# Scale, norm weights, division, epsilon and cosine product in the attention chains of a two-layer mixer kernel

## The chip, the cores and the metric

The kernel runs on one core of a Trainium2 chip. TensorE (PE) multiplies matrices, VectorE (DVE), ScalarE (ACT) and GpSimd (POOL) do the elementwise work, SyncE (SP) issues the loads. The metric is the device time of one execution in microseconds; the median of the runs counts.

## The reference, cut to what matters

Two layers, 256 latent tokens and 256 context tokens of 1024 features. A projection of the normed tokens feeds four branches: a differential attention (a), a pooling (b), a neighbourhood attention (c) and a spatial gating (d). Their outputs are projected, gated, summed and added to the tokens; a SwiGLU follows. The last layer needs only the latents' output. What the change touches is the two attentions:

```
def _rmsnorm(t, g):
    n = t * lax.rsqrt(jnp.mean(t * t, axis=-1, keepdims=True) + EPS)
    return n * g
# a: queries and keys per half head of 64, normed with their weights; latents rotated
aq = _rope(_diff_heads(xcol(OFF_AQ, A_W), ga_q), cos_a, sin_a)
s  = jnp.einsum('bhcqd,bhckd->bhcqk', q, k) * (A_DH ** -0.5)      # 1/8
p  = jax.nn.softmax(s, axis=-1)
a  = p[:, :, 0] - lam * p[:, :, 1]
# c: queries and keys normed, not rotated; bias and mask on the local scores
cq = _rmsnorm(split_c(xcol(OFF_CQ, C_W)), gc_q)
s_loc = jnp.einsum(...) * scale + bias                            # scale = 1/8
p = jax.nn.softmax(jnp.concatenate([s_loc, s_ctx], axis=-1), axis=-1)
out = p_loc @ v_loc + p_ctx @ v_ctx
```

## The kernel before

**Products.** Every large product takes both factors in two parts, hi and lo, and adds hi·hi, lo·hi and hi·lo. `split_weights` (L217 to L232) loads 512 KB of weights on SyncE's queue (`w_raw`), ScalarE rounds them to `w_hi` (L230), VectorE subtracts to get `w_lo` (L127); three buffers of each rotate. `by_token` (L234) keeps activations stationary and streams 512 columns of weights for each of two to four tiles of 128 tokens (products `pt`); `by_feature` (L275) makes the transposed kind (`pf`). All their matmuls have line L124.

**Queries and keys.** `qk_consumer` (L379) takes a finished tile `pt`, 128 tokens by 8 heads of 64. ScalarE copies it to `qn` and squares it, VectorE reduces the squares to `hms` (L386), and `rsqrt_eps` (L147) lets GpSimd add epsilon (L149) and take the power −1/2 (L150), giving `hrs`. Some steps later `scale` multiplies by `hrs` on VectorE (L392). Latents' tiles of branch a are rotated: two products with the sines on VectorE (`qw`, L400), one with the cosines on GpSimd (L401), an addition on VectorE (L402); the norm weights are in these tables (`turn`). All other tiles, 20 of 28, are multiplied by the norm weights `gq` on VectorE (L404). Then `flip` transposes on TensorE (`ps_qT`, L412) and ScalarE copies to `aq`, `ak`, `cq` or `ck` (L413). `stacked` makes from these the parts for the scores (`k_stack`, `q_stack`, `q_low`).

**Attention.** `diff_attention` (L448) takes a head and 128 queries in a step: two score tiles `ps_s`, for each the negated row maximum `mx` on VectorE, its scaling by 1/8 (L470) and the exponential `e` with row sum on ScalarE (L472); VectorE combines the halves (L477), TensorE transposes (`ps_aT`, L485), and later `u` is normed (L511) and transposed (`ps_yT`, L518). `head_attention` (L544) does the same for one score tile `ps_cs` with a bias (L560), maximum `cmx` (L562), scaling (L563), exponential `ce` (L566), reciprocal of the sum `csum` (L567) and the division (L568) on VectorE, then transposes (`ps_pT`, L578), ScalarE's copy `pT` (L579) and the values (`ps_co`).

**Order.** The program is written as steps: `weave` emits a branch's steps with steps of a filler in between (products of another branch, or conditioning: `w_mod_c` on VectorE, L169), and `defer` puts off pieces of a chain by a number of steps. Under the second half of the first layer's neighbourhood attention the filler is the pooling branch, with sums over windows on GpSimd (L855 to L869). The scheduler of the framework then sets the order on each engine; an engine takes its instructions in that order and waits at each for what it needs.

Of the kernel before, what the change touches and what calls it, by code (L numbers as in the profile page):

```python
# [11 lines left out]
F32 = mybir.dt.float32  # L12
F32R = mybir.dt.float32r
AF = mybir.ActivationFunctionType
ALU = mybir.AluOpType
# [4 lines left out]
P = 128  # L20
# [10 lines left out]
# columns of w_in: those of by_token, then those of by_feature  # L31
# [8 lines left out]
def hybrid_block(ctx: ExitStack, tc: tile.TileContext, t: dict, out: bass.AP):  # L40
# [39 lines left out]
    def new_pair(name, n_tok):  # L80
        """hi and lo of [512, n_tok], in two slots or (256 tokens) in one."""
        if n_tok > SEQ:
            return new_slot(name + "_hi", F32R), new_slot(name + "_lo", F32R)
        both = slot.tile([P, 2, 4, SEQ], F32R, tag="S", name=name)
        return both[:, 0], both[:, 1]
# [4 lines left out]
    def weave(main, *fillers):  # L90
        """Emit main, with steps of the fillers ([steps, how many per step of main]) in between."""
# [19 lines left out]
    def flush(most):  # L111
        """Per step of the products: pieces that were put off long enough ago."""
# [34 lines left out]
    def rsqrt_eps(o, ms):  # L147
        n = ms.shape[-1]
        nc.gpsimd.tensor_scalar(o, ms, 1.0, EPS, op0=ALU.mult, op1=ALU.add)  # L149
        nc.gpsimd.tensor_tensor(o, o, half[:, :n], op=ALU.pow)  # L150

# [6 lines left out]
    def conditioning(l, gi):  # L158
        """Two vectors' columns: rows of the transposed w_mod times silu(c), summed in two halves."""
# [23 lines left out]
    def first_load(part):  # L183
        """The columns of w_mod for a quarter of the features of the first shift and scale, in whole slots."""
# [8 lines left out]
    def first_conditioning(part, ws):  # L193
        """A quarter of the features of the first shift and scale; even and odd rows of w_mod side by side."""
# [22 lines left out]
    def split_weights(src, into=None):  # L217
        """A piece [P, nk, nc_] of w in two parts."""
# [15 lines left out]
    def by_token(w, col, act, n_k, tiles, consume, first=None, ahead=False, pairs=False):  # L234
        """[token, column] products: activations stationary, 512 columns of w moving.
        first: tiles to finish before the others, with the parts of w kept on chip."""
# [38 lines left out]
    def by_feature(w, col, act, n_k, n_tok, consume):  # L275
        """[column, token] products: 256 columns of w stationary, activations moving."""
# [20 lines left out]
    def by_feature_pair(cols, act, n_tok):  # L297
        """Two by_feature of 1024 features, the second stream's tokens before the first's,
        with the parts of w kept on chip."""
# [25 lines left out]
    def modulated(l, g_name, v_shift, v_scale, res):  # L325
        """hs, ls and the steps: the squares of both halves and norm of a tile, then put(s, ks) for its stream's features of ks."""
# [5 lines left out]
        def squares(s, i, hf):  # L332
            """Half of a token's mean square, the second half added to the first."""
# [45 lines left out]
    def qk_consumer(name, qk, op, row, which=None, wait=2):  # L379
        def consume(i, ps):  # L380
# [9 lines left out]
            def scale():  # L390
                n3 = n.rearrange("p (g d) -> p g d", g=8)
                nc.vector.tensor_tensor(n3, n3, rs.unsqueeze(2).to_broadcast([P, 8, 64]), op=ALU.mult)  # L392
                if which is not None and i < 2:
# [7 lines left out]
                    nc.gpsimd.tensor_tensor(n3, n3, cg[:, i:i + 1, :].to_broadcast([P, 8, 64]), op=ALU.mult)  # L401
                    nc.vector.tensor_tensor(n, n, w, op=ALU.add)  # L402
                else:
                    nc.vector.tensor_tensor(n3, n3, op["gq"][:, row:row + 1, :].to_broadcast([P, 8, 64]), op=ALU.mult)  # L404
                defer(flip, wait)

            def flip():
# [5 lines left out]
                nc.scalar.copy(qk[name][:, :, i * P:(i + 1) * P], pt.rearrange("p (f n) -> p f n", f=4))  # L413
# [12 lines left out]
    def stacked(qT, kT, hp, n_q):  # L426
        """For heads 2 hp + c, from partitions 64 c on: k_hi and, on the other half, k_lo; q_hi and q_lo on both halves."""
# [675 lines left out]
```

## Time and profile before

| | us |
|---|---|
| median of three runs | 1589.87 (1589.41 to 1590.72) |
| span of the profiled execution | 1588.6 |
| TensorE busy, its matmuls | 1532.6 (96%) |
| VectorE busy | 1024.4 (64%) |
| ScalarE busy | 711.8 (45%) |
| GpSimd busy | 140.3 (9%) |

The span runs from the first to the last instruction of one profiled execution; the rest of the device time lies around it. Busy shares are means over stages of different kinds. The waits of an engine are its idle stretches, put down to the instruction that ended them. A granted clock of 1.00 is TensorE at 2.4 GHz, 0.50 at 1.2 GHz. Matmuls are pipelined, so one that is shown as 0.39 us long is followed by the next after 0.23 us.

### The profile page before, as it was taken

Reading aid. Unit: us, or ns where it says so; the run is one execution under the profiler, and the core shown is the slowest. Engines: PE = TensorE matmul, PEld = TensorE weight load, DVE = VectorE, ACT = ScalarE, POOL = GpSimd, SP = SyncE. Lnnn points to the kernel's source line nnn. Section 1 sums busy time; section 2 is a strip of 40 time slices with the busy share of each in tenths; the row PEclk is TensorE's granted clock in tenths of the full one; section 3 lists DMA queues with packets and bytes.
Section 4 is the critical chain, followed back from the end, with each engine's and each line's share of the span. In section 5 each row is a group of like instructions: output and inputs, shape, how many; then the busy total and the mean of one; then the engine's idle time right before and its main releaser. Section 6 shows DMA issues by size and latency. Waiting matters only on the chain.

```text
span 1588.6 us, 22209 instructions
## 1 busy us (share of the span) xinstructions
PE 1532.6 (96%) x8388; PEld 1300.1 (82%) x8388; DVE 1024.4 (64%) x1957; ACT 711.8 (45%) x1213; POOL 140.3 (9%) x162
## 2 busy tenths in 40 slices
PE   6989999999989999999999999999999999999998
PEld 4778887887767888888888888778978989899897
DVE  2656886556876786577555556567855896655555
ACT  4544463455643233533221233546645675454443
POOL 0220000400050000000000000130012040000000
PEclk9999999999999999999999999999999999999999
DMA  9423333232325565355555554324424535645554
GB/s 343 146 84 128 107 94 106 67 121 77 116 75 184 159 206 179 107 159 176 174 194 171 174 178 167 107 83 143 134 92 133 190 128 183 203 146 184 188 187 144
DMA packets 80988, 235.76 MB, mean 148 GB/s; under 512 B 10560, under 2 KB 13424, under 8 KB 80752
## 3 DMA queue, kind: packets, MB, share of 16 engines
q1 hardware_dynamic: 80880, 234.34, 45.3%
q8 instruction: 66, 1.08, 0.3%
q14 instruction: 42, 0.34, 0.1%
HBM read 232.18 MB, written 2.12 MB: 147 GB/s over the span
## 4 chain that ended last, share of the span: by engine, by line
PE 80%; DVE 10%; POOL 3%; ACT 3%; DMA 2%; issue 2%; SPq 0%; POOLq 0%; ACTq 0%; DVEq 0%
PE pf L124 47%; PE pt L124 26%; POOL hrs L150 2%; DVE w_lo L127 2%; PE ps_u L124 1%; PE ps_co L124 1%; PE ps_pT L578 1%; DVE w_mod_c L169 1%; PE ps_cs L124 1%; PE ps_s L124 1%; ACT w_hi L230 1%; DMA w_mod<-in_w_mod_t 1%; PE ps_nT L359 1%; DVE qn L392 1%; DVE hms L386 1%
## 5 line engine op out<-in xcount | busy, mean ns | idle before, releaser
L230 ACT CAST w_hi<-w_raw 128x1024 fp32r<-128x1024 f32 x308 | 323.5, 1051 | 546.2 <-PE pf L124 212.8
L127 DVE TENSOR_TENSOR w_lo<-w_raw,w_hi 128x1024 fp32r<-128x1024 f32 x308 | 377.6, 1230 | 276.3 <-ACT w_hi L230 272.1
L124 PE MATMUL pf<-h_hi,w_hi 128*128 128x256 f32 (+1 forms) x1344 | 450.2, 336 | 0.2 <-ACT h_hi L367 0.2
L124 PE MATMUL pf<-h_lo,w_hi 128*128 128x256 f32 (+1 forms) x1344 | 449.2, 335 | 0.0
L124 PE MATMUL pf<-h_hi,w_lo 128*128 128x256 f32 (+1 forms) x1344 | 448.7, 334 | 0.2 <-DVE w_lo L127 0.2
L124 PEld LDWEIGHTS pf<-h_lo,w_hi 128*128 128x128 f32 x1344 | 255.5, 190 | 26.3 <-issue 1.2
L124 PEld LDWEIGHTS pf<-h_hi,w_hi 128*128 128x128 f32 x1344 | 255.1, 190 | 26.6 <-ACT h_hi L367 0.7
L124 PEld LDWEIGHTS pf<-h_hi,w_lo 128*128 128x128 f32 x1344 | 255.4, 190 | 25.3 <-DVE w_lo L127 0.4
L169 DVE SCALAR_TENSOR_TENSOR w_mod_c<-w_mod,crow 128x512 f32<-128x512 f32 x256 | 169.3, 694 | 32.5 <-DMA w_mod<-in_w_mod_t 31.3
L124 PE MATMUL pt<-w_lo,h_hi 128*128 128x512 f32 x384 | 152.4, 397 | 6.9 <-DVE w_lo L127 6.9
L124 PE MATMUL pt<-w_hi,hid 128*128 128x512 f32 x496 | 154.3, 390 | 0.0
L124 PE MATMUL pt<-w_hi,h_lo 128*128 128x512 f32 x384 | 151.4, 395 | 1.0 <-DVE h_lo L127 1.0
L124 PE MATMUL pt<-w_hi,h_hi 128*128 128x512 f32 x384 | 152.0, 400 | 0.1
L124 PEld LDWEIGHTS pt<-w_hi,hid 128*128 128x128 f32 x496 | 93.2, 188 | 19.4
L124 PE MATMUL pt<-w_lo,hid 128*128 128x512 f32 x248 | 96.5, 389 | 0.0
L124 PEld LDWEIGHTS pt<-w_lo,h_hi 128*128 128x128 f32 x384 | 72.9, 190 | 23.8 <-DVE w_lo L127 8.7
L124 PEld LDWEIGHTS pt<-w_hi,h_lo 128*128 128x128 f32 x384 | 73.0, 190 | 16.4 <-DVE h_lo L127 1.4
L124 PEld LDWEIGHTS pt<-w_hi,h_hi 128*128 128x128 f32 x384 | 72.9, 190 | 15.3 <-ACT h_hi L367 0.5
L343 POOL TENSOR_TENSOR rs<-rs,half 128x1 f32<-128x1 f32 x14 | 11.2, 803 | 652.4 <-DVE rs L342 646.7
L124 PEld LDWEIGHTS pt<-w_lo,hid 128*128 128x128 f32 x248 | 46.6, 188 | 9.4
L392 DVE TENSOR_TENSOR qn<-qn,hrs 128x512 f32<-128x512 f32 x28 | 21.5, 769 | 43.4 <-POOL hrs L150 43.3
L150 POOL TENSOR_TENSOR hrs<-hrs,half 128x8 f32<-128x8 f32 x28 | 46.9, 1674 | 2.3
(232 smaller groups left out, 2049.3 us busy)
## 6 DMA issues: line engine op xcount, KB each, us to landing
w_raw<-in_w_gu SPq DMA_DIRECT2D x88, 512.0 KB, 3.7
w_mod<-in_w_mod_t SPq DMA_DIRECT2D x160, 256.0 KB, 3.3
w_raw<-in_w_inf SPq DMA_DIRECT2D x80, 512.0 KB, 3.3
w_raw<-in_w_in SPq DMA_DIRECT2D x56, 512.0 KB, 3.4
w_raw<-in_w_down SPq DMA_DIRECT2D x44, 512.0 KB, 3.3
w_raw<-in_w_branch SPq DMA_DIRECT2D x32, 512.0 KB, 3.4
w_mod<-in_w_mod SPq DMA_DIRECT2D x16, 512.0 KB, 9.2
w_raw<-in_w_out SPq DMA_DIRECT2D x16, 512.0 KB, 3.3
```

The costliest lines, as they stand in the source:

```text
L124: nc.tensor.matmul(o, a, b, start=start, stop=stop)
L127: nc.vector.tensor_tensor(o, full, hi.bitcast(F32), op=ALU.subtract)
L150: nc.gpsimd.tensor_tensor(o, o, half[:, :n], op=ALU.pow)
L169: nc.vector.scalar_tensor_tensor(work("w_mod_c"), w, 1.0, crow[:, s, c], op0=ALU.mult, op1=ALU.mult, accum_out=mpart[:, h, v, s, kt:kt + 1])
L230: nc.scalar.copy(hv, rv)
L343: nc.gpsimd.tensor_tensor(rs, rs, half[:, :1], op=ALU.pow)
L359: nc.tensor.transpose(pt[:, u * 256 + i * P:u * 256 + (i + 1) * P], n[s, i][:, (k0 + u) * P:(k0 + u + 1) * P], ident)
L386: nc.vector.tensor_reduce(ms, sq.rearrange("p (g d) -> p g d", g=8), axis=AX.X, op=ALU.add)
L392: nc.vector.tensor_tensor(n3, n3, rs.unsqueeze(2).to_broadcast([P, 8, 64]), op=ALU.mult)
L578: nc.tensor.transpose(pt[:, k * P:(k + 1) * P], e[:, k * P:(k + 1) * P], ident)
```

## The change

Five edits, all in the chains of the two attentions:

- The 1/8 of the scores goes into the queries' norm weights: the first two rows of `gq` (from which the rotation's tables are made) and two columns of a new tile are multiplied by 0.125. The scalings of `mx` and `cmx` and the exponentials' scale fall away, and the bias is no longer multiplied by 8.
- The new tile `gqc` holds the norm weights with features on partitions, for 64 features twice: two loads per layer. Tiles that are not rotated no longer multiply by `gq`; the copy of their transposes becomes an activation with the column of `gqc` as its scale.
- The division of `ce` moves from VectorE to ScalarE.
- Epsilon moves from GpSimd to VectorE, in all uses of `rsqrt_eps`.
- The cosine product moves from GpSimd to VectorE.

```
     def rsqrt_eps(o, ms):
         n = ms.shape[-1]
-        nc.gpsimd.tensor_scalar(o, ms, 1.0, EPS, op0=ALU.mult, op1=ALU.add)
+        nc.vector.tensor_scalar(o, ms, 1.0, EPS, op0=ALU.mult, op1=ALU.add)
         nc.gpsimd.tensor_tensor(o, o, half[:, :n], op=ALU.pow)
...
-                    nc.gpsimd.tensor_tensor(n3, n3, cg[:, i:i + 1, :].to_broadcast([P, 8, 64]), op=ALU.mult)
+                    nc.vector.tensor_tensor(n3, n3, cg[:, i:i + 1, :].to_broadcast([P, 8, 64]), op=ALU.mult)
                     nc.vector.tensor_tensor(n, n, w, op=ALU.add)
-                else:
-                    nc.vector.tensor_tensor(n3, n3, op["gq"][:, row:row + 1, :].to_broadcast([P, 8, 64]), op=ALU.mult)
                 defer(flip, wait)
...
-                nc.scalar.copy(qk[name][:, :, i * P:(i + 1) * P], pt.rearrange("p (f n) -> p f n", f=4))
+                o = qk[name][:, :, i * P:(i + 1) * P]
+                if which is not None and i < 2:
+                    nc.scalar.copy(o, pt.rearrange("p (f n) -> p f n", f=4))
+                else:
+                    nc.scalar.activation(o, pt.rearrange("p (f n) -> p f n", f=4), AF.Copy, scale=op["gqc"][:, row:row + 1])
...
-                nc.vector.tensor_scalar_mul(mx, mx, 0.125)
                 e = awork("e")
-                nc.scalar.activation(e[:, :n_key], sc, AF.Exp, bias=mx, scale=0.125, accum_out=sums[:, 2 * qt + c:2 * qt + c + 1])
+                nc.scalar.activation(e[:, :n_key], sc, AF.Exp, bias=mx, accum_out=sums[:, 2 * qt + c:2 * qt + c + 1])
...
-            nc.vector.tensor_scalar_mul(mx, mx, 0.125)
             e = awork("ce")
             sm1 = asmall("csum", 1)
-            nc.scalar.activation(e[:, :n_key], sc, AF.Exp, bias=mx, scale=0.125, accum_out=sm1)
+            nc.scalar.activation(e[:, :n_key], sc, AF.Exp, bias=mx, accum_out=sm1)
             nc.vector.reciprocal(sm1, sm1)
-            nc.vector.tensor_scalar_mul(e[:, :n_key], e[:, :n_key], sm1)
+            nc.scalar.activation(e[:, :n_key], e[:, :n_key], AF.Copy, scale=sm1)
...
-            nc.vector.scalar_tensor_tensor(b3, b3, 8.0, mask.unsqueeze(1).to_broadcast([P, 12, 64]), op0=ALU.mult, op1=ALU.add)
+            nc.vector.tensor_tensor(b3, b3, mask.unsqueeze(1).to_broadcast([P, 12, 64]), op=ALU.add)
...
             nc.sync.dma_start(gq, t["qk_g"][l:l + 1].to_broadcast([P, 6, 64]))
+            gqc = op["gqc"] = lay.tile([P, 6], F32, tag="gqc", name="gqc")
+            for c in range(2):
+                nc.sync.dma_start(gqc[64 * c:64 * c + 64], t["qk_g"][l].rearrange("r d -> d r"))
+
+            nc.vector.tensor_scalar_mul(gq[:, 0:2], gq[:, 0:2], 0.125)
+            nc.vector.tensor_scalar_mul(gqc[:, 0:5:4], gqc[:, 0:5:4], 0.125)
```

The scheduler sets the order anew. On VectorE, the end of the first layer's query projection in branch a, where three tiles' multiplications by `hrs` stand ahead of the rotation; before:

```order
L386 TENSOR_REDUCE hms<-sq 128x8
L404 TENSOR_TENSOR qn<-qn,gq 128x512
L392 TENSOR_TENSOR qn<-qn,hrs 128x512
L755 TENSOR_TENSOR lpr<-al 128x128
L400 TENSOR_TENSOR qw<-qn,turn 128x16x16
L756 TENSOR_REDUCE lp<-lpr 128x2
L400 TENSOR_TENSOR qw<-qn,turn 128x16x16 x3
L402 TENSOR_TENSOR qn<-qn,qw 128x512
L404 TENSOR_TENSOR qn<-qn,gq 128x512
L758 TENSOR_TENSOR nlam<-lp 128x1
L402 TENSOR_TENSOR qn<-qn,qw 128x512
```

and after:

```order
L392 TENSOR_TENSOR qn<-qn,hrs 128x512
L149 TENSOR_SCALAR hrs<-hms 128x8
L761 TENSOR_TENSOR lpr<-al 128x128
L400 TENSOR_TENSOR qw<-qn,turn 128x16x16
L762 TENSOR_REDUCE lp<-lpr 128x2
L400 TENSOR_TENSOR qw<-qn,turn 128x16x16 x2
L401 TENSOR_TENSOR qn<-qn,turn 128x512
L400 TENSOR_TENSOR qw<-qn,turn 128x16x16
L402 TENSOR_TENSOR qn<-qn,qw 128x512
L764 TENSOR_TENSOR nlam<-lp 128x1
L401 TENSOR_TENSOR qn<-qn,turn 128x512
L765 TENSOR_SCALAR nlam<-nlam 128x1
```

Both products with `gq` are gone, two cosine products (L401) have come, and the fourth multiplication by `hrs` and the second addition stand behind these rows.

On VectorE, the second layer's keys of branch a; before:

```order
L386 TENSOR_REDUCE hms<-sq 128x8
L392 TENSOR_TENSOR qn<-qn,hrs 128x512
L386 TENSOR_REDUCE hms<-sq 128x8
L400 TENSOR_TENSOR qw<-qn,turn 128x16x16 x2
L392 TENSOR_TENSOR qn<-qn,hrs 128x512
L127 TENSOR_TENSOR w_lo<-w_raw,w_hi 128x1024
L402 TENSOR_TENSOR qn<-qn,qw 128x512
```

and after:

```order
L392 TENSOR_TENSOR qn<-qn,hrs 128x512
L386 TENSOR_REDUCE hms<-sq 128x8
L400 TENSOR_TENSOR qw<-qn,turn 128x16x16
L149 TENSOR_SCALAR hrs<-hms 128x8
L400 TENSOR_TENSOR qw<-qn,turn 128x16x16
L127 TENSOR_TENSOR w_lo<-w_raw,w_hi 128x1024
L401 TENSOR_TENSOR qn<-qn,turn 128x512
L392 TENSOR_TENSOR qn<-qn,hrs 128x512
```

The subtraction for `w_lo` has moved ahead of the second tile's multiplication by `hrs`.

On TensorE, the first layer's neighbourhood attention with the pooling branch's products (`pf`) between; before:

```order
L124 MATMUL pf_4076<-h_hi_205,w_lo 128x512
L578 MATMUL ps_pT<-ident,ce 128x128 x2
L124 MATMUL pf_4076<-h_hi_205,w_hi 128x512
L124 MATMUL pf_4076<-h_lo_207,w_hi 128x512
L124 MATMUL pf_4076<-h_hi_205,w_lo 128x512
L578 MATMUL ps_pT<-ident,ce 128x128 x2
L124 MATMUL ps_cs<-k_stack,q_stack 128x512
```

and after:

```order
L578 MATMUL ps_pT<-ident,ce 128x128 x2
L124 MATMUL pf_4004<-h_hi_205,w_lo 128x512
L124 MATMUL pf_4004<-h_hi_205,w_hi 128x512
L124 MATMUL pf_4004<-h_lo_207,w_hi 128x512
L124 MATMUL pf_4004<-h_hi_205,w_lo 128x512
L124 MATMUL pf_4004<-h_hi_205,w_hi 128x512
L578 MATMUL ps_pT<-ident,ce 128x128 x2
L124 MATMUL ps_cs<-k_stack,q_stack 128x512
```

The first two transposes now stand five products ahead of the other two instead of three, and a product of this filler piece is left for after the scores that follow.

On ScalarE at the same place (ScalarE's copies into `pool` belong to the pooling branch); before:

```order
L230 CAST w_hi<-w_raw 128x1024
L566 ACTIVATE ce,csum<-ps_cs,cmx 128x512
L857 COPY pool<-pf_4076 128x2x256
L566 ACTIVATE ce,csum<-ps_cs,cmx 128x512
L579 COPY pT<-ps_pT 128x4x128 x2
L230 CAST w_hi<-w_raw 128x1024
L566 ACTIVATE ce,csum<-ps_cs,cmx 128x512
```

and after:

```order
L566 ACTIVATE ce,csum<-ps_cs,cmx 128x512
L230 CAST w_hi<-w_raw 128x1024
L568 ACTIVATE ce<-ce,csum 128x512
L566 ACTIVATE ce,csum<-ps_cs,cmx 128x512
L863 COPY pool<-pf_4005 128x2x256
L568 ACTIVATE ce<-ce,csum 128x512
L579 COPY pT<-ps_pT 128x4x128 x2
L566 ACTIVATE ce,csum<-ps_cs,cmx 128x512
L568 ACTIVATE ce<-ce,csum 128x512
L566 ACTIVATE ce,csum<-ps_cs,cmx 128x512
```

Each exponential is followed by its division (L568), mostly with one other instruction in between, and once directly.

## Rows read from the trace of the kernel before

**Rows 1.** The page: busy time by engine, and the chain that ended last.

```profile
PE 1532.6 (96%) x8388; PEld 1300.1 (82%) x8388; DVE 1024.4 (64%) x1957; ACT 711.8 (45%) x1213; POOL 140.3 (9%) x162
...
PE 80%; DVE 10%; POOL 3%; ACT 3%; DMA 2%; issue 2%; SPq 0%; POOLq 0%; ACTq 0%; DVEq 0%
```

**Rows 2.** TensorE's waits: line waited for, us in total, times, longest us.

```profile
PE pt L124 <- DVE w_lo L127: 6.9, 5, 2.8
...
PE ps_qT L412 <- DVE qn L402: 4.8, 2, 3.5
PE ps_pT L578 <- DVE ce L568: 3.9, 3, 2.6
PE ps_yT L518 <- DVE u L511: 3.8, 4, 1.2
PE ps_aT L485 <- DVE e L477: 3.1, 6, 1.0
...
PE ps_pT L578 <- DVE cmx L563: 1.7, 2, 0.9
...
PE pt L124 <- DVE h_lo L127: 1.0, 1, 1.0
```

**Rows 3.** TensorE's timeline, 92 to 100 us: start, duration, work, idle before.

```profile
97.05 0.97 PE L412 MATMUL ps_qT<-ident,qn 128*128 128x128 f32 x4 [3.46 <-DVE qn L402]
99.39 1.09 PE L412 MATMUL ps_qT<-ident,qn 128*128 128x128 f32 x4 [1.37 <-DVE nlam L759]
```

**Rows 4.** Windows: length, busy PE PEld DVE ACT POOL, granted clock, DMA share, GB/s.

```profile
69.90:73.30 3.40, 3.40 (x10) 2.61 (x9) 1.53 (x2) 0.00 (x0) 0.00 (x0) 0.50 0.78 246
97.20:104.00 6.80, 5.43 (x17) 4.29 (x17) 6.80 (x15) 1.17 (x2) 0.83 (x1) 0.50 0.34 103
448.80:452.10 3.30, 3.30 (x11) 2.62 (x10) 3.02 (x10) 0.88 (x2) 0.00 (x0) 0.50 0.35 84
```

**Rows 5.** VectorE's timeline, 89 to 99 us.

```profile
89.10 0.69 DVE L392 TENSOR_TENSOR qn<-qn,hrs 128x512 f32<-128x512 f32 x1 [1.81 <-POOL hrs L150]
...
92.79 0.69 DVE L392 TENSOR_TENSOR qn<-qn,hrs 128x512 f32<-128x512 f32 x1 [1.81 <-POOL hrs L150]
...
94.14 2.16 DVE L400 TENSOR_TENSOR qw<-qn,turn 128x256 f32<-128x256 f32 x3
...
96.83 1.75 DVE L404 TENSOR_TENSOR qn<-qn,gq 128x512 f32<-128x512 f32 x1
```

**Rows 6.** GpSimd's timeline in the same stretch.

```profile
91.12 1.64 POOL L150 TENSOR_TENSOR hrs<-hrs,half 128x8 f32<-128x8 f32 x1
94.70 1.32 POOL L401 TENSOR_TENSOR qn<-qn,turn 128x512 f32<-128x512 f32 x1 [1.94 <-DVE qw L400]
```

**Rows 7.** Groups by line and shape: busy us, mean ns, idle before.

```profile
L568 DVE TENSOR_SCALAR ce<-ce,csum 128x512 f32<-128x512 f32 x32 | 18.0, 561 | 0.7
...
L404 DVE TENSOR_TENSOR qn<-qn,gq 128x512 f32<-128x512 f32 x20 | 14.5, 737 | 0.0
L149 POOL TENSOR_SCALAR hrs<-hms 128x8 f32<-128x8 f32 x28 | 13.2, 470 | 128.3 <-DVE hms L386 127.7
L401 POOL TENSOR_TENSOR qn<-qn,turn 128x512 f32<-128x512 f32 x8 | 11.8, 1480 | 8.5 <-DVE qw L400 8.1 <-ACT w_hi L230 0.4
...
L563 DVE TENSOR_SCALAR cmx<-cmx 128x1 f32<-128x1 f32 x48 | 7.1, 148 | 0.6
...
L413 ACT COPY ak<-ps_qT 128x512 f32<-128x512 f32 x8 | 4.6, 585 | 0.8 <-PE ps_qT L412 0.8
...
L520 ACT ACTIVATE ya_hi<-ps_yT,gsub 128x512 fp32r<-128x512 f32 x4 | 2.7, 685 | 8.4 <-PE ps_yT L518 8.4
```

**Rows 8.** VectorE's timeline under the pooling, a division in the first layer.

```profile
446.81 1.47 DVE L568 TENSOR_SCALAR ce<-ce,csum 128x512 f32<-128x512 f32 x1
```

**Rows 9.** The stretch of the first layer's neighbourhood attention before the pooling, as in rows 4.

```profile
331.00:440.00 109.00, 108.40 (x538) 83.85 (x537) 79.11 (x184) 63.51 (x130) 4.19 (x9) 1.00 0.29 94
```

**Rows 10.** Loads: tile, queue, count, KB each, us from issue to landing.

```profile
gsub<-in_a_subln_g SPq DMA_DIRECT2D x2, 0.5 KB, 2.9
```

## The prediction

> **What bounds the kernel now.** I read the engines' busy shares and the chain first, then TensorE's waits by releaser, then the stretches around the long waits, then the groups of the instructions that the change touches. TensorE is busy 1532.6 of 1588.6 us, and the chain that ends last runs for 80% of its length over TensorE and 10% over VectorE [rows 1]. So an edit is worth what it takes from TensorE's 56.0 us of idle time, and from stretches in which TensorE runs at a lower clock; what VectorE or ScalarE gain elsewhere is free time that nobody waits for. The waits list says which idle time the change can reach [rows 2]: w_lo 6.9, the rotated queries or keys 4.8, h_lo 1.0 (all in the projections of the attention branches); u 3.8 and e 3.1 (differential attention); ce 3.9 and cmx 1.7 (neighbourhood attention). A further 1.4 us is released by nlam [rows 3], because the last products of a tile queue beside it on VectorE. Together 26.6 us in 24 waits. The remaining 29 us (start-up, transposes behind the norms, the end) are not touched.
>
> Behind three of these waits TensorE runs at a granted clock of 0.50, the 1.2 GHz level, until 73.3, 104.0 and 452.1 us; before each it had stood idle: in one of the waits for w_lo, in the 4.8 us for qn and nlam, and in the 2.6 us for ce [rows 2 to 4]. At half the rate half of the busy time there is lost: 0.5 × (3.40 + 5.43) = 4.4 us in the projections, 0.5 × 3.30 = 1.65 in the attention [rows 4]. At stake are about 26.6 + 6.1 = 33 us.
>
> **The change part by part.**
>
> **Norm weights into the copy, epsilon and cosine product to VectorE.** The first layer's queries are the example. TensorE ends its products and wants the first rotated tile from 97.05 − 3.46 = 93.6 us, the second one transpose group later; they come at 97.05 and 99.39 [rows 3]. VectorE's chain before that: four times in a row it idles, mostly 1.81 us, for GpSimd's hrs and then multiplies (two of them in [rows 5]); GpSimd takes an epsilon step, 0.47 in the mean, and a power, 1.64 [rows 6, 7]; then VectorE multiplies the sines, GpSimd the cosines (1.32 and longer), which VectorE's sines and the 1.75 us norm product are running beside [rows 5, 6]. After: the norm product of 737 ns goes (20 of them, 14.5 us) and with it the 1.75; epsilon stands behind the reduction on VectorE; the fourth tile's multiplication moves behind the first rotation, as the order shows. The pieces: the third multiplication starts at 89.10; the round trips before it lose GpSimd's epsilon once to three times, 0.5 to 1.4 us, so it ends near 88.4 to 89.3. Then epsilon, lambda's small steps, three sine products, a cosine product, another sine and the first addition: about 0.2 + 0.5 + 1.0 + 0.7 + 0.35 + 0.7 = 3.4, so the first tile is there at 91.8 to 92.7; cosine, the fourth multiplication and the second addition, 2.2 more, put the second at 94.0 to 94.9. TensorE wants them at 93.6 and 94.1 to 94.4. So 4.1 to 4.8 of the 4.8 us go here, with the slow stretch behind them. The keys of the first layer run the same way: VectorE's idling for GpSimd and two norm products stood before the w_lo there.
>
> Epsilon on VectorE has no row; the nearest are the 148 ns of the one-column scaling and GpSimd's 470 [rows 7]. I take 0.2, since it is a small VectorE instruction like the first. The 28 cost 28 × 0.2 = 5.6 us of VectorE time, and the eight cosine products 8 × 0.7 = 5.6 (bounds: the 737 ns of the norm product and GpSimd's 1480 [rows 7]); against that 14.5 go. The w_lo of weights stand in the same queue, so less queue is their gain. In the second layer's keys one w_lo moves ahead of a multiplication, which is the 2.8 us wait. Of 6.9 + 4.8 + 1.4 + 1.0 = 14.1 us I take 13.1 (half of h_lo and a rest of the queries stay), and the 4.4 of the slow stretches: **17.5 us**.
>
> The copy of 20 of the 28 transposes gets a column as its scale: it was 585 ns, and an activation out of PSUM with a column as scale takes 685 [rows 7]. Each lies before the stacking of the keys or queries; +0.1 us × 20 = 2.0 at most, zero where TensorE has products of the next weights.
>
> **1/8 into the weights.** 96 one-column scalings go, 148 ns each [rows 7], and each lay between maximum and exponential. For u and e (6.9 us in 10 waits) a step holds two score tiles, so up to 0.3 us per wait: **3.0 us**. Their mean is 0.7, so the rest stays.
>
> **Division on ScalarE.** VectorE loses 32 × 561 ns (and the 16 of 256 columns). The 2.6 us wait for ce [rows 2] comes from a division that took 1.47 us instead of 0.56 beside GpSimd's pooling and stood behind a conditioning product [rows 8]. With the division on ScalarE it stands behind one exponential, and ScalarE is idle there: the wait and its slow stretch go, 2.6 + 1.65 = **4.3 us**. The other waits for ce and cmx (2.9) I leave; in the second layer the transposes wait for ScalarE too.
> The price is on ScalarE. A division of 512 columns there has no row: bounds 585 (a copy) and 685 (a scaled activation) against 561 on VectorE [rows 7], +0.02 to +0.12 each, 48 × 0.12 = 6.0 if all is on the path. ScalarE was busy 63.5 of 109.0 us of the first layer's attention stretch while TensorE was busy for 108.4 of them [rows 9]; some 24 of the layer's 32 divisions fall in it, and with 0.69 for each ScalarE comes to 80, 73%, so TensorE's products cover most of it. With the copies, 0 to 8.0 us; I take the middle, **−4.0**, since ScalarE's order is fixed and some exponentials will stand behind a division that waits for its reciprocal on VectorE.
>
> The Trainium skill, page "ScalarE: Activation LUTs", section "Rules for kernel authors", advises VectorE and not ScalarE for a plain multiplication; this speaks against moving the division. By the same page's section "What ACT_TABLE_LOAD costs", an activation with one column operand takes about 280 + 0.833 × 512 = 707 ns, an estimate; the row of 685 agrees to 3%, and with 0.71 in place of 0.685 the upper end would be 9 instead of 8.
>
> **New loads.** Two more small loads per layer on SyncE's queue, of 4-byte elements. The nearest row is gsub, 2.9 us to landing [rows 10]; these have three times its elements, so 3 to 6 us. VectorE reads them first at about 44 us, after loads issued around 33, so nothing waits; if it did, it is a few us once. In the second layer they are due during long products. Zero, with +3 in the range.
>
> **Sum.** 17.5 + 3.0 + 4.3 − 4.0 = 20.8 us. The profiled span was 1588.6, and 1.3 us of the median time of 1589.87 lie outside it; that part stays. 1588.6 − 20.8 + 1.3 = **1569.1 us**. About 0.2%, 3.2 us, is what a measurement of this kernel can tell from no change.
>
> **The rivals.**
> - **Only the projections pay.** The transposes in the attentions are issued a few products earlier than before (the order shows it under the pooling), so they may find e and ce no earlier than now. Then 3.0 + 4.3 are not gained: 1589.9 − 17.5 + 3 = 1575 us. For it: the ten waits for u and e are short, 0.7 us in the mean, less than the few products by which a transpose moves.
> - **Slower: ScalarE waits in order for reciprocals.** Before, only VectorE stood behind a reciprocal; now ScalarE does, and exponentials, casts of the weights and copies queue behind a division. If each of 48 holds TensorE for 0.8 us (a VectorE product of 0.7 ahead of the reciprocal), 38 us come on top: 1569 + 38 = 1607. It turns slower than before from 20.8 / 48 = 0.43 us per division. Against it: the order puts a weight cast or an exponential between most pairs, and TensorE has the filler's products.
> - **VectorE becomes the holder.** If the cosine products and epsilons stand ahead of the w_lo and hold it as long as the norm products did, the 17.5 stay: 1589.9 − 7.3 + 4 = 1587 us.
> - **The slower engine counts in full.** All 48 divisions and 20 copies lie on the path, and the attention gains nothing: 1589.9 − 17.5 + 8.0 = 1580 us. The rule of the page "ScalarE: Activation LUTs" in the Trainium skill would be borne out by this; no trace of before shows it, since VectorE's 561 is only 0.12 better and rises to 1.47 beside pooling.
>
> **How the numbers follow.** Forecast 0.52 (1560 to 1573), only the projections 0.23, ScalarE in full 0.11, VectorE the holder 0.06, slower 0.08. Range 1560 to 1584: below, the 4 us of loss fall away and the other waits for ce, cmx, u and e shrink; above, it takes in the second and fourth rival and the late loads. Faster by over 0.2%: 0.52 + 0.23 + 0.11 = 0.86; within: 0.06; slower: 0.08.
>
> **What would show it.** In the profile after, w_lo and the rotated tile should have left TensorE's waits, and the stretches of 0.50 clock near 73, 104 and 452 us should be gone; VectorE's idle time before the multiplication by hrs should shrink. If instead ScalarE rises in TensorE's waits (transposes released by ce of ScalarE, or scores released by the exponential), the price of the division was too low. If VectorE's w_lo stays there, the third rival is right. The prediction is wrong if the time is over 1584 or if the waits outside the attentions grow, which would mean that the new order of the whole program counts for more than these steps.

## The result, and the profile after

The changed kernel takes 1564.69 us (median of four, 1563.21 to 1567.43) against 1590.13 for the kernel before (now four runs): a ratio of 0.9838, 95% interval 0.9825 to 0.9850, 25.4 us less. Forecast were 1569, with a range of 1560 to 1584. The profiled execution took 1563.21 us, 1561.4 of it span, 27.2 us less span than before.

The page's busy times and chain, as [rows 1]:

```profile
PE 1523.9 (98%) x8388; PEld 1296.0 (83%) x8388; DVE 982.7 (63%) x1847; ACT 740.5 (47%) x1261; POOL 117.2 (8%) x112
...
PE 87%; DVE 5%; ACT 3%; POOL 2%; issue 1%; DMA 1%; POOLq 0%; SPq 0%; ACTq 0%; DVEq 0%
```

TensorE is idle for 1561.4 − 1523.9 = 37.5 us instead of 56.0, and busy for 8.7 us less with the same 8388 matmuls. Of the 8.7, 6.1 are the half of the busy time that was lost in the three stretches at half the clock [rows 4]. The rest fits the number of waits, an estimate: a matmul ahead of a wait shows its whole 0.39 us instead of 0.23, 0.16 more, and the list of waits has 15 entries less (30 for 45), 2.4 us. VectorE's share of the chain has halved. TensorE's waits now, as [rows 2]:

```profile
PE pt L124 <- DVE w_lo L127: 4.2, 4, 2.6
...
PE ps_yT L519 <- DVE u L512: 2.1, 3, 0.9
PE ps_pw L124 <- ACT ce L566: 1.3, 1, 1.3
PE ps_aT L486 <- DVE e L478: 1.2, 2, 0.7
PE ps_aT L486 <- ACT th L728: 0.9, 1, 0.9
...
PE pt L124 <- DVE h_lo L127: 0.5, 1, 0.5
PE ps_qT L410 <- DVE qn L402: 0.4, 1, 0.4
```

The 5.6 us for ce and cmx on VectorE have no row any more, the 4.8 for the rotated tile are 0.4, and nlam's 1.4 are gone. Two waits have come on ScalarE, 2.2 us together; three others on ScalarE (for `pT` and `yb`), also 2.2 us together, are gone. The first layer's queries on TensorE's timeline, as [rows 3], and the keys' remaining wait:

```profile
67.15 0.50 PE L124 MATMUL pt<-w_lo,h_hi 128*128 128x512 f32 x1 [1.09 <-DVE w_lo L127]
...
89.70 0.60 PE L410 MATMUL ps_qT<-ident,qn 128*128 128x128 f32 x4
90.66 0.63 PE L410 MATMUL ps_qT<-ident,qn 128*128 128x128 f32 x4 [0.36 <-DVE qn L402]
```

The windows behind them, and that of the first layer's neighbourhood attention up to the pooling's products, show what the clock did, as [rows 4, 9] (length, busy PE PEld DVE ACT POOL, granted clock):

```profile
67.15:73.30 6.15, 6.15 (x32) 5.19 (x32) 2.35 (x3) 0.62 (x1) 0.00 (x0) 1.00 0.76 244
90.66:104.00 13.34, 13.15 (x63) 10.82 (x64) 8.31 (x14) 7.79 (x14) 0.00 (x0) 1.00 0.62 198
...
323.34:457.13 133.79, 133.38 (x665) 102.36 (x664) 84.43 (x176) 91.52 (x191) 25.30 (x26) 1.00 0.31 101
```

All three stretches of 0.50 are gone. In the last line ScalarE is busy for 68% with the divisions, and TensorE still has 99.7% of the time.

By stages, from the start of the first instruction of each kind on TensorE's timeline of both profiles:

| from .. to | before, us | after, us | difference |
|---|---|---|---|
| first layer: keys' first transposes .. first scores | 65.1 | 54.9 | −10.2 |
| differential attention, to the first transposes of ck | 163.0 | 162.0 | −1.1 |
| projection of the neighbourhood attention | 43.4 | 41.7 | −1.8 |
| neighbourhood attention, merge, to the next norm | 301.2 | 293.2 | −7.9 |
| last layer: keys' transposes .. first scores | 52.2 | 49.4 | −2.8 |
| differential attention, to the first transposes of ck | 107.2 | 106.5 | −0.7 |
| projection of the neighbourhood attention | 33.2 | 33.2 | 0.0 |
| neighbourhood attention, to the next norm | 160.5 | 159.0 | −1.4 |
| all else, to the end of the last matmul | 658.2 | 657.0 | −1.2 |

And the groups of the instructions that the change made, for the terms of the sum (columns as [rows 7]):

```profile
L568 ACT ACTIVATE ce<-ce,csum 128x512 f32<-128x512 f32 x32 | 22.9, 723 | 4.0 <-DVE csum L567 4.0
...
L401 DVE TENSOR_TENSOR qn<-qn,turn 128x512 f32<-128x512 f32 x8 | 5.4, 681 | 0.0
...
L415 ACT ACTIVATE ck<-ps_qT,gqc 128x512 f32<-128x512 f32 x8 | 5.2, 682 | 0.0
L149 DVE TENSOR_SCALAR hrs<-hms 128x8 f32<-128x8 f32 x28 | 4.7, 168 | 0.6
```

### The profile page after: what moved, and what is told of

It is laid out like the page before. It is cut to its first block, busy times and chain, and to the rows that moved or that the text cites. A ratio compares the mean times of both kernels' runs of the same rounds, so it can differ in the third digit from the quotient of the medians.

```text
span 1561.4 us, 22070 instructions
## 1 busy us (share of the span) xinstructions
PE 1523.9 (98%) x8388; PEld 1296.0 (83%) x8388; DVE 982.7 (63%) x1847; ACT 740.5 (47%) x1261; POOL 117.2 (8%) x112
## 4 chain that ended last, share of the span: by engine, by line
PE 87%; DVE 5%; ACT 3%; POOL 2%; issue 1%; DMA 1%; POOLq 0%; SPq 0%; ACTq 0%; DVEq 0%
PE pf L124 50%; PE pt L124 29%; PE ps_co L124 1%; PE ps_cs L124 1%; POOL hrs L150 1%; PE ps_pT L578 1%; DVE w_lo L127 1%; PE ps_u L124 1%; PE ps_s L124 1%; ACT w_hi L230 1%; PE ps_qT L410 1%; PE ps_nT L359 1%; DMA w_mod<-in_w_mod 1%; PE ps_aT L486 0%; DVE w_mod_c L169 0%
## 5 line engine op out<-in xcount | busy, mean ns | idle before, releaser
L124 PEld LDWEIGHTS pf<-h_lo,w_hi 128*128 128x128 f32 x1344 | 255.0, 190 | 25.4 <-issue 0.4
L124 PEld LDWEIGHTS pf<-h_hi,w_lo 128*128 128x128 f32 x1344 | 254.9, 190 | 25.4 <-issue 0.8
L150 POOL TENSOR_TENSOR hrs<-hrs,half 128x8 f32<-128x8 f32 x28 | 52.5, 1876 | 140.1 <-DVE hrs L149 127.6
L986 ACT CAST hid<-silu 128x512 fp32r<-128x512 f32 (+1 forms) x44 | 22.5, 512 | 48.0 <-DVE silu L984 48.0
```

Of the source, the lines that this page charges most:

```text
L124: nc.tensor.matmul(o, a, b, start=start, stop=stop)
L986: nc.scalar.copy(hd, sl[j])
```

## The experiments

The theory is the prediction's: TensorE waited for chains on VectorE and GpSimd, and each edit shortens one of them at the place where its waits stood. Its rivals are that one or two edits do all of it, that ScalarE pays for the division, and that the scheduler's other order is what gains. Each run is compared by its ratio to the kernel before on the same chip; the difference of two ratios times 1590 gives us against the changed kernel's 0.9838. Intervals are 2 to 5 us wide on either side, and the changed kernel's own is 2, so differences under 3 to 4 us stay open. The stages that are given beside a time are those of one profiled execution. No run keeps the scheduler's order and changes an engine alone: where order and duration are told apart below, the timelines do it.

### Each edit undone by itself

**Division back on VectorE.**

```
-            nc.scalar.activation(e[:, :n_key], e[:, :n_key], AF.Copy, scale=sm1)
+            nc.vector.tensor_scalar_mul(e[:, :n_key], e[:, :n_key], sm1)
```

> The changed kernel with the division of ce back on VectorE, all else as changed (1564.7 us). Theory (the division was held on VectorE by pooling and conditioning, and ScalarE does it for nothing): TensorE's waits for ce and cmx of the first layer come back, 4 to 6 us with a slow stretch behind the longest, about 1570 us. Rival (ScalarE pays what VectorE saved): 1562 to 1566 us, with the waits that ScalarE ends gone.

Measured: 1570.79 us, ratio 0.9877 (0.9860 to 0.9893), 6.2 us more. TensorE's waits in the stretch of the first layer's neighbourhood attention, and the division that the longest waits for, on VectorE's timeline:

```profile
PE ps_pT L578 <- DVE ce L568: 2.7, 2, 2.3
```

```profile
428.57 2.02 DVE L127 TENSOR_TENSOR w_lo<-w_raw,w_hi 128x1024 fp32r<-128x1024 f32 x1
430.51 1.29 DVE L568 TENSOR_SCALAR ce<-ce,csum 128x512 f32<-128x512 f32 x1
```

The wait for ce is back at the place where the pooling runs on GpSimd, again behind a slow instruction of VectorE's queue. Up to the pooling's products the stage is 3.5 us longer, in the last layer it is 0.8; 1.8 more are one wait for a conditioning column behind the attention, which five of the fourteen profiles have, with 0.3 to 1.8 us. The slow stretch that was expected behind the longest wait did not come. The rest of the theory holds, and the price on ScalarE is smaller than what VectorE's queue costs.

**1/8 back on the maxima.**

```
+                nc.vector.tensor_scalar_mul(mx, mx, 0.125)
-                nc.scalar.activation(e[:, :n_key], sc, AF.Exp, bias=mx, accum_out=...)
+                nc.scalar.activation(e[:, :n_key], sc, AF.Exp, bias=mx, scale=0.125, accum_out=...)
```

(the same for `cmx`, and the bias times 8 again)

> The changed kernel with the 1/8 back as 96 scalings of the maxima and as the exponentials' scale. Theory (each score loses 0.15 to 0.3 us of latency, and TensorE waits in the differential attention for e and u): about 3 us more, 1568 us, with more waits for e and u. Rival (the scheduler's other order gained them): 1563.5 to 1566 us.

Measured: 1570.86 us, ratio 0.9870 (0.9855 to 0.9884), 5.1 us more. Its waits:

```profile
PE ps_aT L487 <- DVE e L479: 3.0, 6, 1.1
...
PE ps_yT L520 <- DVE u L513: 1.8, 2, 1.1
PE ps_pT L580 <- ACT ce L570: 1.6, 1, 1.6
PE pf L124 <- ACT w_hi L230: 1.1, 1, 1.1
```

The waits for e are as many and as long as in the kernel before (3.1 in 6, [rows 2]). But that is only 1.8 us more than the changed kernel's 1.2; by stages, the two differential attentions are 0.1 and 1.4 us longer, the two neighbourhood attentions 1.4 and 2.7. There ScalarE is waited for longer: ce and w_hi, 2.7 us and a further 0.5 for ce elsewhere, where the changed kernel has 1.3 for ce. What holds the first of them stands on ScalarE's timeline:

```profile
434.34 0.72 ACT L570 ACTIVATE ce<-ce,csum 128x512 f32<-128x512 f32 x1 [1.75 <-DVE csum L569]
```

ScalarE stands for 1.75 us before a division, whose reciprocal comes on VectorE behind two conditioning products of 1.50 and 1.55 us, and TensorE waits for 1.56 of them. With the division on ScalarE and the scalings on VectorE this one reciprocal comes late, as it does in the run with the division alone below. What the last layer's 2.7 us come from was not traced further.

**Norm weights back on VectorE.**

```
+                else:
+                    nc.vector.tensor_tensor(n3, n3, op["gq"][:, row:row + 1, :].to_broadcast([P, 8, 64]), op=ALU.mult)
...
-                    nc.scalar.activation(o, pt.rearrange(...), AF.Copy, scale=op["gqc"][:, row:row + 1])
+                    nc.scalar.copy(o, pt.rearrange(...))
```

(and the 1/8 in the row of `gq` for the queries of branch c)

> The changed kernel with the norm weights of the 20 tiles back on VectorE as products and the transposes copied without a scale. Theory (VectorE's queue of these 14.5 us stood ahead of the w_lo that TensorE wanted): waits for w_lo and the rotated tiles grow, 1569 to 1573 us. Rival (GpSimd's round trips were the holder, the products stood in VectorE's idle time): 1564 to 1567 us.

Measured: 1567.57 us, ratio 0.9851 (0.9836 to 0.9865), 2.1 us more, which the intervals don't settle; by the ratio it is 1566 us, in the rival's range and below the theory's. The waits of the stretch from 60 to 130 us:

```profile
PE pt L124 <- DVE w_lo L127: 1.7, 1, 1.7
PE ps_qT L412 <- DVE qn L402: 1.3, 1, 1.3
PE ps_qT L412 <- DVE nlam L767: 0.8, 1, 0.8
```

In the changed kernel these are 1.3, 0.4 and none. With the slow stretch behind them the first layer's stage is 3.7 us longer; the last layer's differential attention and the start of the projection behind it are 2.1 us shorter, since a w_lo stands there in a better place of the order (1.09 us of waiting instead of 2.58, below). So the edit of 14.5 us of VectorE time is the one that brought least in these runs.

**Epsilon back on GpSimd.**

```
-        nc.vector.tensor_scalar(o, ms, 1.0, EPS, op0=ALU.mult, op1=ALU.add)
+        nc.gpsimd.tensor_scalar(o, ms, 1.0, EPS, op0=ALU.mult, op1=ALU.add)
```

> The changed kernel with epsilon back on GpSimd, 28 steps of 0.47 us and their handovers. Theory (GpSimd's round trips hold the first layer's keys and queries): each round trip 0.3 to 0.5 us longer, three in a row ahead of the rotated queries, 1.0 to 1.5 us of waits and a slow stretch behind them: 1566 to 1569 us. Rival (the round trips are hidden once the norm weights are gone): 1564 to 1565.5 us.

Measured: 1574.99 us, ratio 0.9899 (0.9884 to 0.9914), 9.7 us more: the largest of the five, and more than either theory said. First VectorE's timeline of this run, then that of the changed kernel:

```profile
83.92 0.69 DVE L392 TENSOR_TENSOR qn<-qn,hrs 128x512 f32<-128x512 f32 x1 [1.09 <-POOL hrs L150]
...
86.42 0.69 DVE L392 TENSOR_TENSOR qn<-qn,hrs 128x512 f32<-128x512 f32 x1 [1.21 <-POOL hrs L150]
88.93 0.69 DVE L392 TENSOR_TENSOR qn<-qn,hrs 128x512 f32<-128x512 f32 x1 [1.81 <-POOL hrs L150]
```

```profile
82.29 0.69 DVE L392 TENSOR_TENSOR qn<-qn,hrs 128x512 f32<-128x512 f32 x1 [0.81 <-POOL hrs L150]
...
84.87 0.69 DVE L392 TENSOR_TENSOR qn<-qn,hrs 128x512 f32<-128x512 f32 x1 [1.23 <-POOL hrs L150]
...
87.89 0.68 DVE L402 TENSOR_TENSOR qn<-qn,qw 128x512 f32<-128x512 f32 x1
...
89.23 0.68 DVE L392 TENSOR_TENSOR qn<-qn,hrs 128x512 f32<-128x512 f32 x1
```

With epsilon on GpSimd a round trip takes 2.50 us (83.92 to 86.42 to 88.93), with epsilon on VectorE 2.58 (82.29 to 84.87): it is not shorter, since epsilon then waits in VectorE's queue behind the multiplication. Only the first round trip is, 3.03 us (from 79.26) for 3.81 (from 80.11), and that isn't what is missing: counted from the keys' first transposes, the third multiplication by hrs starts after 20.1 us in the changed kernel and after 19.5 here. What differs is the order. On GpSimd the fourth multiplication, for a tile that isn't wanted yet, stands ahead of the rotation again and holds it for one more round trip; on VectorE it stands behind the first addition, where its power is long there. The rotated tiles come late by

```profile
92.70 0.63 PE L410 MATMUL ps_qT<-ident,qn 128*128 128x128 f32 x4 [2.02 <-DVE nlam L764]
95.17 1.09 PE L410 MATMUL ps_qT<-ident,qn 128*128 128x128 f32 x4 [1.84 <-DVE qn L402]
```

and the stage is 3.3 us longer; the last layer's keys are 2.4 longer, by a w_lo wait of 2.31 us that the changed kernel doesn't have. There the w_lo stands behind the second multiplication by hrs again, which waits for GpSimd; in the changed kernel it stands ahead of it:

```profile
1031.53 0.69 DVE L392 TENSOR_TENSOR qn<-qn,hrs 128x512 f32<-128x512 f32 x1 [1.53 <-POOL hrs L150]
...
1032.74 1.22 DVE L127 TENSOR_TENSOR w_lo<-w_raw,w_hi 128x1024 fp32r<-128x1024 f32 x1
```

So 5.7 us stand at the two places where the order of the rotated tiles and of this w_lo changed. The differential attention behind it is 2.4 us longer, with a stretch at half the clock from 1176.7 to 1180.1. The 1.9 in the last neighbourhood attention are no effect of the order: all engines have there the order of the changed kernel, and two other runs of which this is true, the next one and one of the last section, are 1.9 and 3.2 us longer in it too, and others are not. Why is open.

**Cosine product back on GpSimd.**

```
-                    nc.vector.tensor_tensor(n3, n3, cg[:, i:i + 1, :].to_broadcast([P, 8, 64]), op=ALU.mult)
+                    nc.gpsimd.tensor_tensor(n3, n3, cg[:, i:i + 1, :].to_broadcast([P, 8, 64]), op=ALU.mult)
```

> The changed kernel with the cosine product back on GpSimd, eight times about 1.3 to 1.6 us against 0.68 on VectorE, and a handover each way. Theory (the chain of the rotated tiles is what TensorE waits for): the two queries of the first layer come 1 to 2 us later, with VectorE slowed beside GpSimd, and the keys' w_lo too: 1568 to 1571 us, waits for the rotated tile back. Rival (with the norm weights and epsilon gone there is slack): 1564 to 1566 us.

Measured: 1570.81 us, ratio 0.9875 (0.9853 to 0.9897), 5.9 us more. GpSimd's and VectorE's timelines of the first layer's queries:

```profile
86.15 1.95 POOL L150 TENSOR_TENSOR hrs<-hrs,half 128x8 f32<-128x8 f32 x1 [0.89 <-DVE hrs L149]
88.07 2.53 POOL L401 TENSOR_TENSOR qn<-qn,turn 128x512 f32<-128x512 f32 x2
```

```profile
89.39 1.76 DVE L402 TENSOR_TENSOR qn<-qn,qw 128x512 f32<-128x512 f32 x1 [1.59 <-POOL qn L401]
```

The cosine product starts only after the fourth tile's power on GpSimd, and the first addition, which the second cosine product runs beside, takes 1.76 us instead of 0.68. VectorE's order is nearly the changed kernel's here, so this edit pays by its own durations: 3.4 us in the first layer's stage, 1.6 in the last layer's keys. The profile has 2.9 more in the last layer's two attentions, where the order is the changed kernel's: the 1.9 named above, and a slow stretch behind a wait for w_lo that the changed kernel has as well.

### The disputed price, and parts alone

**A second division.**

```
             nc.scalar.activation(e[:, :n_key], e[:, :n_key], AF.Copy, scale=sm1)
+            nc.scalar.activation(e[:, :n_key], e[:, :n_key], AF.Copy, scale=1.0)
```

> The changed kernel with a second activation in place, times 1, behind each of the 48 divisions: 48 x 0.5 to 0.72 us, 31 us more work on ScalarE and 0.6 us more in each chain. Theory (ScalarE's time beside the attention is free and a step of the chain has room): 0 to 6 us more, up to 1571 us. Rival (the divisions lie on the path, so a second one costs as much as the first): 20 to 33 us more, 1585 us and above.

Measured: 1567.50 us, ratio 0.9853 (0.9830 to 0.9875), 2.4 us more. ScalarE's groups:

```profile
L568 ACT ACTIVATE ce<-ce,csum 128x512 f32<-128x512 f32 x32 | 22.9, 722 | 3.1 <-DVE csum L567 3.1
...
L569 ACT ACTIVATE ce<-ce 128x512 f32<-128x512 f32 x32 | 20.0, 630 | 0.2
```

With the 16 of 256 columns, 26.6 us more of ScalarE's work cost 2.4 us, about a tenth of it, and the intervals don't tell that from nothing. The first layer's stage took 0.6 us more, the last layer's attention 1.8. So a microsecond of ScalarE's work here costs a small part of one, and the mechanism that would have made the change slower, divisions that hold TensorE one by one, shows once, with 1.05 us.

**The division alone**, on the kernel before.

> The kernel before with the division on ScalarE and nothing else changed. Theory (it pays by itself, at VectorE's pooling stretch): the waits for ce go, 4 to 7 us less than before, 1583 to 1586 us. Rival (it pays only with the shorter chain of the maximum): 1588 to 1591 us.

Measured: 1587.51 us, ratio 0.9982 (0.9967 to 0.9996), 2.9 us less, short of the theory's 4 to 7. The first layer's stage is 4.9 us shorter, but a wait that the forecast's slower rival described is there once:

```profile
445.23 0.72 ACT L568 ACTIVATE ce<-ce,csum 128x512 f32<-128x512 f32 x1 [1.75 <-DVE csum L567]
```

```profile
446.00 0.66 PE L578 MATMUL ps_pT<-ident,ce 128*128 128x128 f32 x4 [1.51 <-ACT ce L568]
```

ScalarE stands for 1.75 us before a division, since the reciprocal stands on VectorE behind two conditioning products, and TensorE waits for 1.51 of them. It is the place at which the run with the 1/8 undone has its 1.56. In the changed kernel ScalarE still stands for 1.33 us before one division, but no matmul waits for it. The rest of the missing gain is one stretch at half the clock (last section), 1.6 us in the last layer's keys, and 0.9 in the last layer's neighbourhood attention.

**Epsilon alone**, on the kernel before.

> The kernel before with epsilon on VectorE and nothing else changed. If the edits of the projection chain add up, it brings what its undoing costs, 6 to 10 us: 1581 to 1585 us. Rival (with products and cosines still in the chain the tiles come late all the same, and only together do they arrive in time): 1586 to 1590 us.

Measured: 1578.69 us, ratio 0.9920 (0.9891 to 0.9949), 12.7 us less (8.1 to 17.3): half of the whole change from one line, and more than the 6 to 10 of the theory. The stage of the first layer's queries is 6.0 us shorter, with all products and cosines still in the chain. The rival is out. Here too the fourth multiplication stands behind the rotation.

**The attention's edits alone** (1/8 and division; the norm weights, epsilon and cosine as before).

> The changed kernel with epsilon and the cosine product back on GpSimd and the norm weights back on VectorE, so that the 1/8 and the division on ScalarE are left. If the attention and the projection edits are independent: the waits of the attentions stay away, the stages of the projections are as long as before, 10 to 12 us less than before in all, 1578 to 1581 us. Rival (the attention's gain needs the projections' other order): 1583 us and above.

Measured: 1584.09 us, ratio 0.9949 (0.9933 to 0.9964), 8.1 us less, between the two forecasts. The waits for ce and cmx on VectorE are gone, and the neighbourhood stage is 293.98 us long, as in the changed kernel (293.24). The two edits undone singly cost 11.3. The profiled execution had 1.7 us more before its first product, and two stretches at half the clock that the kernel before doesn't have, so this may be what independence gives; it isn't settled.

### Can the rest be had?

What is left are waits for w_lo: 1.09 at 67 us, 2.58 at 1167 us. The first stands behind a multiplication by hrs whose power took 4.49 us on GpSimd instead of 1.64, in the changed kernel:

```profile
60.74 4.49 POOL L150 TENSOR_TENSOR hrs<-hrs,half 128x8 f32<-128x8 f32 x1
```

```profile
65.26 0.69 DVE L392 TENSOR_TENSOR qn<-qn,hrs 128x512 f32<-128x512 f32 x1 [1.53 <-POOL hrs L150]
65.87 1.22 DVE L127 TENSOR_TENSOR w_lo<-w_raw,w_hi 128x1024 fp32r<-128x1024 f32 x1
```

VectorE ran rotation steps, two cosine products among them, without a pause until 63.73; the power ended 1.5 us after that. With the cosine product back on GpSimd the power at this place takes 1.64 again and the wait is 0.79, with 0.39 for a rotated tile ahead of it.

**Longer deferral.**

```
-        wait = 2 if last else 1
+        wait = 3 if last else 2
```

> The changed kernel with the steps by which the multiplication by hrs and the transposes are put off raised from 1 to 2 in the first layer and from 2 to 3 in the last. Theory (what is left are w_lo that stand on VectorE behind a multiplication that waits for GpSimd's power): the waits for w_lo, 4.2 us, fall by half or more, 1561 to 1563 us. Rival (the end of a projection has no later step to put it off to, so it comes late there): 1565 to 1570 us.

Measured: 1568.79 us, ratio 0.9866 (0.9842 to 0.9889), 4.5 us more. The wait at 67 us is gone, and a later one has come:

```profile
93.76 0.50 PE L124 MATMUL pt<-w_lo,h_hi 128*128 128x512 f32 x1 [2.55 <-DVE w_lo L127]
```

The lateness has moved to the next weights, with a slow stretch behind it (95.2 to 98.6). In the last layer the long wait stays (2.59 for w_lo).

**VectorE's norm weights for the last layer's neighbourhood tiles.** An argument `onv` is true for `ck` and `cq` of the last layer, and there the product with `gq` and the plain copy stand again.

> The changed kernel with the norm weights on VectorE for the last layer's neighbourhood queries and keys alone (six products). Theory (there the copy's scale only changed the order, so that a w_lo stands behind one more multiplication that waits for GpSimd): the last layer's wait of 2.6 us for w_lo falls to 1.1, about 2 us less than the changed kernel: 1562 to 1563.5 us. Rival (it costs as much in the chain): 1564 to 1566 us.

Measured: 1565.31 us, ratio 0.9828 (0.9805 to 0.9851). TensorE's wait there, in this run and, below it, in the changed kernel:

```profile
1165.68 0.50 PE L124 MATMUL pt<-w_lo,h_hi 128*128 128x512 f32 x1 [1.08 <-DVE w_lo L127]
```

```profile
1166.62 0.50 PE L124 MATMUL pt<-w_lo,h_hi 128*128 128x512 f32 x1 [2.58 <-DVE w_lo L127]
```

The wait falls as expected, and the stages around it are 2.1 us shorter. By the ratio the time is 1.6 us less than the changed kernel's, about what was expected, but that is inside the intervals. In the profiled execution the last neighbourhood attention, with the order of the changed kernel, took 3.2 us more, with a stretch at half the clock near 1265 us.

**The same, with the first layer's keys put off by two steps.**

> The kernel of the run before this one with the first layer's keys of branch a put off by two steps instead of one. Theory (the first layer's w_lo of the queries then stands ahead of the keys' last multiplications): the 1.1 us wait for w_lo near 67 us goes and nothing comes near 91, 1 to 2 us less: 1560 to 1562 us. Rival (as with the longer deferral of all chains, a later w_lo is late): 1563 to 1567 us.

Measured: 1565.63 us (1562.20 to 1571.14), ratio 0.9836 (0.9806 to 0.9867). The wait at 67 us moves to 91 us and grows to 2.53. Neither version is faster than the changed kernel by more than the intervals.

## Why the prediction was right

Sign, size and the main mechanism held: the time fell by 25.4 us, 20.8 were forecast, and most of the waits that the sum rests on went. How the gain is shared among the edits did not hold, and that the sum is so near is in part luck: two errors of opposite sign, projections too high by 2.7 us and attentions too low by 7.8 (11.1 us by stages, 3.0 + 4.3 − 4.0 forecast), partly cancel in it. Term by term:

- **Projections, 17.5 forecast.** The three stages are 10.2 + 1.8 + 2.8 = 14.8 us shorter. The queries of the first layer came as replayed (0.36 of 4.8 us left), and the two slow stretches went. What failed is the full recovery of w_lo: 4.2 of 6.9 stay, and the one in the last layer's second projection grew from 1.50 to 2.58, because the new order puts three multiplications that wait for GpSimd ahead of it, where two stood before.
- **How it comes about there was partly wrong.** The prediction took 0.5 to 1.4 us from the round trips. From the first to the third multiplication by hrs the queries took 5.83 us before (83.27 to 89.10) and 5.61 after (79.26 to 84.87), 0.2 less. It read from the order that the fourth multiplication moves behind the rotation; that epsilon on VectorE is what brings this, it did not say. So for epsilon the rival of the experiments, the other order, is what gains. It set epsilon's 5.6 us of VectorE time against the 14.5 of the norm weights and gave these the gain; undone, epsilon costs 9.7, the cosine product 5.9, and the norm weights 2.1. Epsilon itself was 168 ns, 0.2 were taken; the cosine product 681 ns, 0.7 taken.
- **1/8, 3.0 forecast.** Undone it costs 5.1. The differential attentions gave 1.8 by stages, or 3.2 without the second projection's w_lo, whose longer wait (2.58 + 0.34 for 1.50) falls into one of them. In the run with the 1/8 undone, 4.1 us of the loss stand in the neighbourhood attentions, where the prediction gave it nothing.
- **Division, 4.3 forecast and −4.0 for its price.** This is the term that was mis-sized. The neighbourhood stages gave 7.9 + 1.4 = 9.3 us instead of 0.3, by this edit and the 1/8 together; undone by itself the division costs 6.2. All waits for ce and cmx on VectorE went, not only the longest; and most of the price isn't there: 26.6 us of added work on ScalarE cost 2.4. A division is slower on ScalarE, 723 ns against 561 [rows 7], above the bounds of 585 to 685 that were taken.
- **The rivals.** ScalarE standing before a reciprocal held TensorE once each in two runs, 1.51 us with the division alone and 1.56 with the 1/8 undone, far from 0.43 per division in 48. The other three gave 1575 to 1587 us, above all four runs of the changed kernel, and the waits that two of them leave for e, ce and the rotated tiles are short or gone.
- **New loads** cost nothing: they landed 3.2 us after issue, and in the first layer VectorE scales the new tile at 44.1 us without a wait for it; in the last it waited 0.31 us, with nobody behind it.

The rule of the Trainium skill, page "ScalarE: Activation LUTs", section "Rules for kernel authors", to take VectorE for a plain multiplication, agrees with the trace for the single instruction (723 ns on ScalarE, 561 on VectorE). For the time of the kernel it didn't decide: the division undone cost 6.2 us. By the Trainium skill, same page, section "What ACT_TABLE_LOAD costs", an estimate of 707 ns for the division was 2% under the measured 723.

## What to carry to other kernels

Price an instruction by who waits behind it on its engine, not by its duration: the edit of a 0.17 us step brought most, for the larger part because it changed what stands ahead of the rotation and of one w_lo, and the one that freed 14.5 us of VectorE brought least. Whether work on an engine with idle time is free can be seen by doubling it there. Where a scheduler sets the order, read for each edit what now stands ahead of an instruction that is waited for, though nobody waits for it yet itself. And compare stages whose order did not change: where they differ, look at other runs of the same order before it is put down to the edit.

## What the runs showed of the hardware

- VectorE and GpSimd can slow each other. VectorE's addition of 0.68 us took 1.76 beside GpSimd's product (the run with the cosine on GpSimd), its division of 0.56 took 1.29 (division undone) and 1.47 (kernel before) beside the pooling. The other way, GpSimd's power of 1.64 us took 2.54 us beside a w_lo of VectorE, in the changed kernel:

```profile
1165.52 2.54 POOL L150 TENSOR_TENSOR hrs<-hrs,half 128x8 f32<-128x8 f32 x1 [0.89 <-DVE hrs L149]
```

```profile
1165.35 1.22 DVE L127 TENSOR_TENSOR w_lo<-w_raw,w_hi 128x1024 fp32r<-128x1024 f32 x1
```

Not each time: a power at 1024.41 us of the same execution, which began 0.10 us ahead of a w_lo, took 1.68, and the w_lo beside it 1.23.
- The same wait can or can't be followed by the 1.2 GHz level. Behind a wait of 2.8 us for the same w_lo, the kernel before ran at full clock (first line) and the one with the division alone at 0.56 (second line), which fits half as many matmuls into the 3 us:

```profile
1050.80:1053.80 3.00, 3.00 (x16) 2.49 (x16) 2.35 (x4) 0.00 (x0) 1.64 (x1) 1.00 0.56 175
```

```profile
1045.90:1048.90 3.00, 3.00 (x8) 2.38 (x9) 2.33 (x4) 0.00 (x0) 1.67 (x1) 0.56 0.52 175
```

The attention's edits alone have it there too (0.50 behind 2.76 us). Each such stretch costs 1.5 to 2 us, and another lies in the start of four of the profiled executions (23 to 26.5 us at a clock of 0.51 in the run with epsilon undone). That is as much as some edits bring, and why the smaller differences here stay open.
